# Dilated-attention scores as half-height products, with phase ends and first transfers reordered

## Chip, cores and metric

One core of a Trainium2 chip runs the whole program. The metric is device time in microseconds (us) of one execution; lower is better. Before the change three runs took 2113.09, 2116.16 and 2117.09 us, so the median is 2116.16.

## What is computed

The input x has 512 tokens of 1024 features. Two blocks follow each other.

The first block has two layers. In each, `p = rms_norm(x) @ w_in` gives the inputs of a latent attention (8 heads) and of a dilated attention, both gated with silu, and `x = x + concat(a, b) @ w_out`. The dilated attention has three groups of 8 heads of 64 features, with (window, dilation) of (128, 1), (512, 4) and (2048, 16). For each group

```
s = where(|qpos - kpos| <= half, q . k * 64 ** -0.5, -inf)
o, lse = softmax(s) @ v, logsumexp(s)
```

and the three outputs are mixed with `softmax(lse)` over the groups. A rotary embedding turns the first 16 features of each head of q and k.

The second block is an FFN, a mixer (a gated linear recurrence beside a window attention with sinks) and another FFN, each closed by an rms norm and added to the residual. All matrices are f32, and the result must be near the f32 reference.

## The kernel before

**Layout.** Activations lie with features on the 128 partitions and the 512 tokens along the row, so a 1024-feature matrix is eight tiles of 128 x 512. Weights stream in as 128 x 1024 pieces (`weights`, lines 129 to 143): a transfer on SP's queue, a cast to F32R on ACT (`hi`), and the rest `lo` on DVE. A product at nearly f32 precision is three F32R products, hi x hi, hi x lo and lo x hi (`mm3`, line 147). F32R runs in one pass, F32 in two.

**Order.** A scheduler places the instructions of each engine when the kernel is built. It goes by priorities (`high_priority`), by the order of the program and by modelled times; on the chip each engine then runs its list in order. `behind` adds an order without a wait. PSUM has eight banks of 128 x 512; `banks` (line 87) says which of them serve which kind of tile (`mm` projections, `s` scores, `t` transposes, `o` values), and each kind takes its banks in turn.

**Dilated attention** (in `layer`, lines 455 to 469). Heads go in four pairs, and a pair's two heads are the two halves of the 128 partitions. `dil_proj` makes q and k of three groups with six projections of 24 products. For group 0 and each head, the query tile `Qs[h]` holds the hi part on the head's own 64 partitions and the lo part on the other 64, and the keys `Kh[h]`, `Kl[h]` hold the head's keys twice, copied by eight transfers on SP's queue (line 702). So one product over 128 partitions sums hi and lo. For groups 1 and 2 the key tile `KP` has for each head its keys on its own half and zeros on the other (lines 709 to 712), so that the full query tile meets one head alone. `dil_scores` then makes, for each of four query blocks n and two heads h, one bank `s`: 256 columns of group 0 (lines 731 and 732, F32R) and 128 each of groups 1 and 2 (line 734, F32). DVE adds the mask and takes the maximum (line 739), and ACT takes the exponential (line 742). There is one `s` bank and three `t` banks. `dil_finish` scales, transposes (line 779) and copies (line 780) the probabilities, in turns put between the products of the next pair's last projection, and multiplies them with the values (line 784), head by head onto 64 columns of the array. The last pair of a layer is finished in `out`, among the first products of `w_out`.

**Phase ends** (`finish`, lines 279 to 334). The last output tiles (two in `end` and in `mixer`, one in `ffn`) are made in two halves of 256 tokens, A and B, in the same PSUM bank. `take` squares and copies a half; `stats` sums the squares with products against ones; `norm` runs a chain of small DVE operations for the reciprocal root; `spread` transposes it into a row R; `update` applies it, and the next phase's first projections (`follow`) run on half A while B is still being finished. `stats(0)` and `norm(0)` stand ahead of B's products in the program, `spread(0)` among the last tile's.

**Start.** WARM products on a tile of ones run first. SP's queue loads the vector table `vecs`, the x tile 0, then the weights and x tiles 4 to 7; ACT's queue loads x tiles 1 to 3. `take_x` casts an x tile on ACT, takes the rest on DVE, and squares it on ACT.

**Window attention** (`swa`, lines 1039 to 1053). Four tiles of values V, 24 products each, are made first; after the second the row R is made from `rstd` by four transposes, and keys and queries are scaled by R.

Of the kernel before, what the change touches and what calls it, by code (L numbers as in the profile page):

```python
# [22 lines left out]
P = 128  # L23
D = 1024
KT = 8
# [7 lines left out]
WARM = 6  # L33
# [11 lines left out]
class Kern:  # L45
    def __init__(self, ctx, tc, a, out):
# [18 lines left out]
        with tc.high_priority(1000):  # L65
            nc.sync.dma_start(self.vecs, a["vecs"])
# [212 lines left out]
    def finish(self, ms, prod, take, acc, update, srcs):  # L279


        pss = [self.psum() for _ in ms]
# [3 lines left out]
        def products(part, mid=None):  # L286
            for m, ps in zip(ms, pss):
                prod(m, ps, part, mid if m == ms[-1] else None)
            for m, ps in zip(ms, pss):
                take(m, ps, part)  # L290
# [17 lines left out]
        stats(0)  # L308
        norm(0)
        products(B, lambda: spread(0))  # L310
# [31 lines left out]
class Block1:  # L342
    def __init__(self, k, es):
# [12 lines left out]
        for kt in range(KT):  # L356
            x = self.u("x", F32)
            with tc.high_priority(1000 if kt < 4 else 0):
                (nc.scalar if 0 < kt < 4 else nc.sync).dma_start(x, a["xT"][kt])
            k.take_x(kt, x, k.vcol("norm_g0", kt), acc, sq=x)  # L360
# [13 lines left out]
    def layer(self, L):  # L374
# [84 lines left out]
        k.banks(mm=(0, 1, 2), s=(3,), t=(4, 5, 6), o=(7,))  # L459
# [211 lines left out]
    def dil_proj(self, L, pr, between=()):  # L671
# [4 lines left out]
        for g in range(3):  # L676
            for qk in range(2):
# [6 lines left out]
                if g == 0 and qk == 0:  # L684
                    ve.tensor_add(m1, m1, sh)
                    Qs = [self.q2("Qs", F32R) for _ in range(2)]
                    for h in range(2):
                        b, b2 = slice(64 * h, 64 * h + 64), slice(64 - 64 * h, 128 - 64 * h)
                        q = Qs[h].rearrange("p (t r i) -> p r t i", t=4, r=4)
                        m = m1.rearrange("p (r t i) -> p r t i", r=4, t=4)  # L690
                        nc.scalar.copy(q[b], m[b])
                        ve.tensor_sub(q[b2], m[b], q[b].bitcast(F32))
                elif g == 0:
                    ve.tensor_add(m1, m1, sh)
                    Kh, Kl = [[self.u("K0") for _ in range(2)] for _ in range(2)]
                    both = self.u("K0h"), self.u("K0l")
                    k.split(*both, m1)
                    for src, dst in zip(both, (Kh, Kl)):
                        for h in range(2):
                            b = slice(64 * h, 64 * h + 64)  # L700
# [189 lines left out]
def ffn(k, acc, lead, n, hd, after, srcs):  # L890
# [5 lines left out]
    with k.tc.tile_pool(name=f"ffn{n}", bufs=FT, reuse_waits="tile") as gp:  # L896
# [14 lines left out]
        def prod(m, ps, part, mid=None):  # L911
            for kt in range(FT):
                if mid and kt == FT // 2:
                    mid()
# [472 lines left out]
```

## Time and profile before

| | us |
|---|---|
| median of 3 runs | 2116.16 |
| profiled execution | 2112.34 |
| span of the profile | 2110.6 |
| PE busy | 2082.5 |
| DVE busy | 1328.4 |
| ACT busy | 963.3 |
| POOL busy | 94.8 |

The span goes from the first to the last instruction; the profiled execution took 1.74 us more than that. PE is the matmul engine, PEld its weight loads, DVE the vector engine, ACT the scalar engine, POOL the general one, SP an engine that mainly issues transfers. The time of a matmul in a row is from its start to the end of its last result; matmuls overlap, so their pitch is read from one start to the next.

### The profile page before, as it was taken

Reading aid. Unit: us, or ns where it says so; the run is one execution under the profiler, and the core shown is the slowest. Engines: PE = TensorE matmul, PEld = TensorE weight load, DVE = VectorE, ACT = ScalarE, POOL = GpSimd, SP = SyncE. Lnnn points to the kernel's source line nnn. Section 1 sums busy time; section 2 is a strip of 40 time slices with the busy share of each in tenths; the row PEclk is TensorE's granted clock in tenths of the full one; section 3 lists DMA queues with packets and bytes.
Section 4 is the critical chain, followed back from the end, with each engine's and each line's share of the span. In section 5 each row is a group of like instructions: output and inputs, shape, how many; then the busy total and the mean of one; then the engine's idle time right before and its main releaser. Section 6 shows DMA issues by size and latency. Waiting matters only on the chain.

```text
span 2110.6 us, 30554 instructions
## 1 busy us (share of the span) xinstructions
PE 2082.5 (99%) x11602; PEld 1763.0 (84%) x11602; DVE 1328.4 (63%) x2965; ACT 963.3 (46%) x1753; POOL 94.8 (4%) x350
## 2 busy tenths in 40 slices
PE   8999999999999999999999999999999999999997
PEld 7888889888888898788888889777888888888887
DVE  5866874856767757676555226866788748555323
ACT  5754444544664535543233224655577444223221
POOL 0000211100001201100000000000000000000001
PEclk9999999999999999999999999999999999999999
DMA  4323333433223343244222323322222434322221
GB/s 170 97 66 94 100 93 108 131 120 114 68 81 91 90 124 112 77 140 149 100 92 99 100 98 107 116 81 70 75 89 97 148 106 155 100 94 96 100 99 61
DMA packets 83780, 216.76 MB, mean 103 GB/s; under 512 B 9873, under 2 KB 28977, under 8 KB 83633
## 3 DMA queue, kind: packets, MB, share of 16 engines
q1 hardware_dynamic: 80896, 210.88, 31.1%
q10 hardware_dynamic: 2736, 3.93, 0.5%
q8 instruction: 91, 1.49, 0.3%
q14 instruction: 57, 0.46, 0.1%
HBM read 190.92 MB, written 13.37 MB: 97 GB/s over the span
## 4 chain that ended last, share of the span: by engine, by line
PE 90%; DVE 5%; ACT 2%; DMA 1%; issue 1%; SPq 0%; POOL 0%; DVEq 0%; ACTq 0%
PE ps L149 25%; PE ps L151 25%; PE ps L150 25%; PE ps L177 4%; PE ps L582 1%; PE ps L573 1%; PE ps L734 1%; PE ps L784 1%; PE ps L779 1%; PE ps L556 1%; DVE wl L142 1%; PE ps L557 1%; PE ps L558 1%; PE ps L1135 1%; PE ps L1119 0%
## 5 line engine op out<-in xcount | busy, mean ns | idle before, releaser
L141 ACT CAST wh<-wr 128x1024 fp32r<-128x1024 f32 (+2 forms) x341 | 343.4, 1009 | 682.8 <-PE ps L150 549.2
L149 PE MATMUL ps<-xh,wh 128*128 128x512 f32 x1496 | 592.0, 396 | 0.0
L142 DVE TENSOR_TENSOR wl<-wr,wh 128x1024 fp32r<-128x1024 f32 (+2 forms) x341 | 398.5, 1171 | 301.6 <-ACT wh L141 301.0
L150 PE MATMUL ps<-xl,wh 128*128 128x512 f32 x1496 | 587.4, 393 | 0.0
L151 PE MATMUL ps<-xh,wl 128*128 128x512 f32 x1496 | 587.3, 393 | 0.0
L151 PEld LDWEIGHTS ps<-xh,wl 128*128 128x128 f32 x1496 | 281.4, 188 | 56.4 <-issue 0.6
L149 PEld LDWEIGHTS ps<-xh,wh 128*128 128x128 f32 x1496 | 281.5, 188 | 54.6 <-issue 1.5
L150 PEld LDWEIGHTS ps<-xl,wh 128*128 128x128 f32 x1496 | 281.6, 188 | 52.7 <-issue 0.2
L149 PE MATMUL ps<-gh,wh 128*128 128x512 f32 (+1 forms) x540 | 199.3, 369 | 1.5 <-ACT f L939 1.5
L151 PE MATMUL ps<-gh,wl 128*128 128x512 f32 (+1 forms) x540 | 197.7, 367 | 0.7 <-DVE wl L142 0.7
L150 PE MATMUL ps<-gl,wh 128*128 128x512 f32 (+1 forms) x540 | 197.8, 366 | 0.5 <-DVE gl L191 0.5
L149 PE MATMUL ps<-wh,xh 128*128 128x256 f32 (+1 forms) x416 | 119.3, 287 | 0.2 <-ACT V L662 0.2
L150 PE MATMUL ps<-wl,xh 128*128 128x256 f32 (+1 forms) x416 | 118.9, 286 | 0.0
L151 PE MATMUL ps<-wh,xl 128*128 128x256 f32 (+1 forms) x416 | 118.8, 286 | 0.0
L149 PEld LDWEIGHTS ps<-gh,wh 128*128 128x128 f32 x540 | 101.9, 189 | 19.0 <-ACT f L939 1.9
L151 PEld LDWEIGHTS ps<-gh,wl 128*128 128x128 f32 x540 | 101.9, 189 | 18.0 <-DVE wl L142 1.6
L150 PEld LDWEIGHTS ps<-gl,wh 128*128 128x128 f32 x540 | 101.9, 189 | 16.9 <-DVE gl L191 0.9
L903 DVE TENSOR_TENSOR x<-ps,R 128x512 f32<-128x512 f32 x44 | 30.4, 690 | 98.4 <-PE ps L151 98.4
L901 DVE TENSOR_TENSOR x<-ps,R 128x512 f32<-128x512 f32 x44 | 30.4, 691 | 82.5 <-PE ps L151 81.2
L149 PEld LDWEIGHTS ps<-wh,xh 128*128 128x128 f32 x416 | 79.6, 191 | 1.5 <-ACT V L662 0.6
L150 PEld LDWEIGHTS ps<-wl,xh 128*128 128x128 f32 x416 | 79.5, 191 | 0.4 <-issue 0.2
L151 PEld LDWEIGHTS ps<-wh,xl 128*128 128x128 f32 x416 | 79.5, 191 | 0.4 <-issue 0.2
(303 smaller groups left out, 3247.5 us busy)
## 6 DMA issues: line engine op xcount, KB each, us to landing
wr<-in_ffn_w SPq DMA_DIRECT2D x132, 512.0 KB, 3.4
wr<-in_w_dqk SPq DMA_DIRECT2D x48, 512.0 KB, 3.6
wr<-in_w_dv SPq DMA_DIRECT2D x20, 512.0 KB, 3.5
wr<-in_w_out SPq DMA_DIRECT2D x16, 512.0 KB, 3.6
wr<-in_w_bgate SPq DMA_DIRECT2D x16, 512.0 KB, 3.5
hd<-h SPq DMA_DIRECT2D x48, 128.0 KB, 2.1
h<-hd SPq DMA_DIRECT2D x24, 256.0 KB, 5.5
wr<-in_w_gatea SPq DMA_DIRECT2D x8, 512.0 KB, 3.9
```

The lines of the kernel that those rows point to most:

```text
L141: nc.scalar.copy(hi[:, b:e], w[:, b:e])
L142: nc.vector.tensor_sub(lo[:, b:e], w[:, b:e], hi[:, b:e].bitcast(F32))
L149: first = mm(out, lhsT=wh, rhs=xh, start=start, stop=False)
L150: mm(out, lhsT=wh, rhs=xl, start=False, stop=False)
L151: return first, mm(out, lhsT=wl, rhs=xh, start=False, stop=stop)
L177: self.begin(mm(ps[:, part], lhsT=w[i][:, c], rhs=x[kt][:, part], start=start, stop=kt == KT - 1 and x is self.xl), ps.offset, start)
L556: mm(s, lhsT=qh[0:96, c], rhs=Kh[0:96, h, :], start=True, stop=False)
L557: mm(s, lhsT=qh[0:96, c], rhs=Kl[0:96, h, :], start=False, stop=False)
L558: mm(s, lhsT=ql[0:96, c], rhs=Kh[0:96, h, :], start=False, stop=True)
L573: turned[0] = inst(nc.tensor.transpose(t[:, j * P:(j + 1) * P], p[:, j * P:(j + 1) * P], k.ident))
L901: nc.vector.tensor_mul(x1, ps1, R)
L903: nc.vector.tensor_mul(x3, ps3, R)
```

## The change

Group 0's queries and keys are kept as hi and lo tiles with both heads on their own halves, and a score is three F32R products over 64 partitions: hi x hi, lo x hi, hi x lo. Groups 1 and 2 use the plain query and key tiles, one F32 product over 64 partitions for each head. The doubled keys, their eight transfers, the zero-filled tiles and their memsets are gone. Products are issued for two query blocks at once, alternating between the heads' halves, the second block first. Scores get four banks, of which two are shared with the transposes, which have two instead of three.

In `finish` a single last tile gets a bank for each half; sums and small chain of half A move among B's products, and the spread further back. In the first transfers `vecs` goes to ACT's queue, x tiles 2 and 3 to SP's without their priority, and the handling of x tile 0 gets priority; WARM goes from 6 to 8. In `swa` the row R is made after the third values tile. The changed `mtile` call below is that of `end`; the one of `mixer` differs in the names alone. The changed loop over kt is that of `ffn`, and the last lines are those of `swa`.

```diff
-WARM = 6
+WARM = 8
...
-            nc.sync.dma_start(self.vecs, a["vecs"])
+            nc.scalar.dma_start(self.vecs, a["vecs"])
...
     def finish(self, ms, prod, take, acc, update, srcs):
-        pss = [self.psum() for _ in ms]
+        pss = [(p, p) if len(ms) > 1 else (p, self.psum()) for p in (self.psum() for _ in ms)]
...
-        def products(part, mid=None):
+        def products(part, works=()):
+
+            for i, m in enumerate(ms):
+                prod(m, pss[i][part == B], part, works if len(ms) == 1 else works[i:i + 1])
             for m, ps in zip(ms, pss):
-                prod(m, ps, part, mid if m == ms[-1] else None)
-            for m, ps in zip(ms, pss):
-                take(m, ps, part)
+                take(m, ps[part == B], part)
...
         products(A)
-        stats(0)
-        norm(0)
-        products(B, lambda: spread(0))
+        products(B, (lambda: (stats(0), norm(0)), lambda: spread(0)))
...
             x = self.u("x", F32)
-            with tc.high_priority(1000 if kt < 4 else 0):
-                (nc.scalar if 0 < kt < 4 else nc.sync).dma_start(x, a["xT"][kt])
-            k.take_x(kt, x, k.vcol("norm_g0", kt), acc, sq=x)
+            with tc.high_priority(1000 if kt < 2 else 0):
+                (nc.scalar if kt == 1 else nc.sync).dma_start(x, a["xT"][kt])
+            with tc.high_priority(0 if kt else 500):
+                k.take_x(kt, x, k.vcol("norm_g0", kt), acc, sq=x)
...
-        k.banks(mm=(0, 1, 2), s=(3,), t=(4, 5, 6), o=(7,))
+        k.banks(mm=(0, 1, 2), s=(3, 6, 4, 5), t=(4, 5), o=(7,))
...
-                if g == 0 and qk == 0:
-                    ve.tensor_add(m1, m1, sh)
-                    Qs = [self.q2("Qs", F32R) for _ in range(2)]
-                    for h in range(2):
-                        b, b2 = slice(64 * h, 64 * h + 64), slice(64 - 64 * h, 128 - 64 * h)
-                        q = Qs[h].rearrange("p (t r i) -> p r t i", t=4, r=4)
-                        m = m1.rearrange("p (r t i) -> p r t i", r=4, t=4)
-                        nc.scalar.copy(q[b], m[b])
-                        ve.tensor_sub(q[b2], m[b], q[b].bitcast(F32))
-                elif g == 0:
-                    ve.tensor_add(m1, m1, sh)
-                    Kh, Kl = [[self.u("K0") for _ in range(2)] for _ in range(2)]
-                    both = self.u("K0h"), self.u("K0l")
-                    k.split(*both, m1)
-                    for src, dst in zip(both, (Kh, Kl)):
-                        for h in range(2):
-                            b = slice(64 * h, 64 * h + 64)
-                            for b2 in (slice(0, 64), slice(64, 128)):
-                                nc.sync.dma_start(dst[h][b2, :].bitcast(F32), src[b, :].bitcast(F32))
-                elif qk == 0:
-                    q = self.q2("Q12", F32)
-                    ve.tensor_add(q, m1, sh)
-                    Q12.append(q)
+                if g:
+                    z = self.q2("Q12", F32) if qk == 0 else self.u("K12", F32)
+                    ve.tensor_add(z, m1, sh)
+                    (K12 if qk else Q12).append(z)
+                    continue
+                ve.tensor_add(m1, m1, sh)
+                if qk:
+                    K0 = self.u("K0h"), self.u("K0l")
+                    k.split(*K0, m1)
                 else:
-                    kp = self.k4("KP", F32)
-                    nc.gpsimd.memset(kp[64:128, 0, :], 0.0)
-                    nc.gpsimd.memset(kp[0:64, 1, :], 0.0)
-                    ve.tensor_add(kp[0:64, 0, :], m1[0:64, :], sh[0:64, :])
-                    ve.tensor_add(kp[64:128, 1, :], m1[64:128, :], sh[64:128, :])
-                    K12.append(kp)
+                    Q0 = self.q2("Q0h", F32R), self.q2("Q0l", F32R)
+                    k.split(*(z.rearrange("p (t r i) -> p r t i", t=4, r=4) for z in Q0),
+                            m1.rearrange("p (r t i) -> p r t i", r=4, t=4))
...
+        rows = slice(0, 64), slice(64, 128)
+
+        def scores(n, ss, first):
+
+            c = slice(n * P, (n + 1) * P)
+
+            def win(z):
+                return z.rearrange("p (r i) -> p r i", r=4)[:, :, WIN[n]:WIN[n] + 64]
+
+            for i, (q, kk) in enumerate(((qh, kh), (ql, kh), (qh, kl))):
+                for s, b in zip(ss, rows):
+                    ins = mm(s[:, 0:256], lhsT=q[b, c], rhs=win(kk)[b], start=i == 0, stop=i == 2)
+                    first = k.behind(inst(ins), first)
+            for g in range(2):
+                for s, b in zip(ss, rows):
+                    ins = mm(s[:, 256 + g * P:256 + (g + 1) * P], lhsT=Q12[g][b, c], rhs=K12[g][b, c], start=True, stop=True)
+                    first = k.behind(inst(ins), first)
+            return first
+
+        two = {}
         for n in range(4):
-            c = slice(n * P, (n + 1) * P)
-            for h in range(2):
-                s = k.bank("s")
-                win = [z[h].rearrange("p (r i) -> p r i", r=4)[:, :, WIN[n]:WIN[n] + 64] for z in (Kh, Kl)]
-                mm(s[:, 0:256], lhsT=Qs[h][:, c], rhs=win[0], start=True, stop=False)
-                mm(s[:, 0:256], lhsT=Qs[h][:, c], rhs=win[1], start=False, stop=True)
-                for g in range(2):
-                    mm(s[:, 256 + g * P:256 + (g + 1) * P], lhsT=Q12[g][:, c], rhs=K12[g][:, h, c], start=True, stop=True)
+            if n % 2 == 0:
+                two = {m: [k.bank("s") for h in range(2)][::-1] for m in (n, n + 1)}
+                first = None
+                rows = rows[::-1]
+                for m in (n + 1, n):
+                    first = scores(m, two[m], first)
+                rows = rows[::-1]
+            ss = two[n][::-1]
+            for h, s in enumerate(ss):
...
-            k.mtile(ws[m], 0, gh, gl, range(KT), ps, part=part, between=[mid] if mid else ())
+            k.mtile(ws[m], 0, gh, gl, range(KT), ps, part=part, between=[lambda: None, *works])
...
             for kt in range(FT):
-                if mid and kt == FT // 2:
-                    mid()
+                for work in works[kt // 10:kt // 10 + 1] if kt % 10 == 5 else ():
+                    work()
...
-            if t == 1:
+            if t == 2:
                 k.R = k.row(rstd, "R")
```

## Rows read from the trace of the kernel before

**Rows 1.** The page: busy time per engine, and the chain that ended last by engine.

```profile
PE 2082.5 (99%) x11602; PEld 1763.0 (84%) x11602; DVE 1328.4 (63%) x2965; ACT 963.3 (46%) x1753; POOL 94.8 (4%) x350
...
PE 90%; DVE 5%; ACT 2%; DMA 1%; issue 1%; SPq 0%; POOL 0%; DVEq 0%; ACTq 0%
```

**Rows 2.** Groups by line, shapes apart; columns as in part 5 of the page.

```profile
L734 PE MATMUL ps<-KP,Q 128*128 128x128 f32 x256 | 39.6, 275 | 0.9 <-DVE KP L711 0.9
...
L731 PE MATMUL ps<-K,Qs 128*128 128x256 f32 x64 | 18.6, 291 | 0.3 <-DVE mx L739 0.2
...
L779 PEld LDWEIGHTS ps<-ident,p 128*128 128x128 f32 x256 | 31.6, 140 | 8.4 <-DVE p L777 0.4
...
L784 PEld LDWEIGHTS ps<-PT,V 128*64 128x64 f32 x512 | 27.8, 137 | 1.3 <-issue 1.3
```

**Rows 3.** Timeline of PE, one score tile: start, us, engine, line, operation, count.

```profile
220.39 0.28 PE L731 MATMUL ps<-K,Qs 128*128 128x256 f32 x1
220.50 0.28 PE L732 MATMUL ps<-K,Qs 128*128 128x256 f32 x1
220.62 0.61 PE L734 MATMUL ps<-KP,Q 128*128 128x128 f32 x4
220.98 0.47 PE L151 MATMUL ps<-xh,wl 128*128 128x512 f32 x1
221.30 0.39 PE L149 MATMUL ps<-xh,wh 128*128 128x512 f32 x1
```

**Rows 4.** Timeline of PE, the end of layer 0: transposes, value products, output projection.

```profile
427.81 1.47 PE L779 MATMUL ps<-ident,p 128*128 128x128 f32 x12
429.21 3.71 PE L784 MATMUL ps<-PT,V 128*64 128x128 f32 x64
432.86 0.50 PE L149 MATMUL ps<-gh,wh 128*128 128x512 f32 x1
433.20 0.40 PE L150 MATMUL ps<-gl,wh 128*128 128x512 f32 x1
```

**Rows 5.** Groups by line, DVE and ACT around the dilated scores.

```profile
L739 DVE CUSTOM_DVE_ANT_0 p<-ps,mask 128x256 f32<-128x256 f32 x128 | 49.0, 420 | 20.3 <-PE ps L734 20.1
...
L780 ACT COPY PT<-ps 128x512 f32<-128x512 f32 x64 | 37.3, 589 | 33.2 <-PE ps L779 33.1
...
L712 DVE TENSOR_TENSOR KP<-m,sh 64x512 f32<-64x512 f32 x16 | 11.0, 689 | 0.4
L705 DVE TENSOR_TENSOR Q<-m,sh 128x512 f32<-128x512 f32 x16 | 11.0, 687 | 0.1
...
L711 DVE TENSOR_TENSOR KP<-m,sh 64x512 f32<-64x512 f32 x16 | 10.8, 674 | 0.0
```

**Rows 6.** Busy time by engine, 212.8 to 270, dilated stage: stretch, us, busy (count).

```profile
212.80:270.00 57.20, 57.04 (x345) 47.77 (x344) 46.61 (x137) 27.91 (x60) 11.59 (x38) 1.00 0.30 89
```

**Rows 7.** Timeline of PE, layer 1, the last pair's first scores; the wait in brackets.

```profile
852.68 0.46 PE L734 MATMUL ps<-KP,Q 128*128 128x128 f32 x2 [0.87 <-DVE KP L711]
```

**Rows 8.** Timeline of PE, the ends of Block1 and of the second FFN.

```profile
919.01 0.61 PE L223 MATMUL ps<-ones,sq 128*128 128x1 f32 x4 [0.25 <-DVE sq L251]
...
2089.10 0.28 PE L151 MATMUL ps<-gh,wl 128*128 128x256 f32 x1
2090.12 0.39 PE L149 MATMUL ps<-gh,wh 128*128 128x256 f32 x1 [0.74 <-ACT f L939]
```

**Rows 9.** Timeline of ACT and PE, the first ten microseconds.

```profile
5.84 0.40 ACT L141 CAST wh<-wr 128x256 fp32r<-128x256 f32 x1 [3.61 <-DMA wr<-in_w_lat]
...
8.05 0.72 ACT L190 ACTIVATE xh<-x,vecs 128x512 fp32r<-128x512 f32 x1
...
8.82 1.65 PE L177 MATMUL ps<-xh,wh 128*128 128x512 f32 x3 [4.85 <-ACT xh L190]
```

**Rows 10.** Timeline of PE, the mixer's window attention, before the row R.

```profile
1322.93 0.28 PE L151 MATMUL ps<-wh,xl 128*128 128x256 f32 x1
1325.44 0.65 PE L232 MATMUL ps<-ident,rstd 128*128 128x128 f32 x4 [2.23 <-DVE rstd L213]
```

More of the change, by code (lines that the diff above doesn't have):

```diff
@@ L714, in dil_proj @@
-        return Qs, Kh, Kl, Q12, K12
+                if g:
[7 more added lines that the diff above has]
+                    k.split(*K0, m1)
+                else:
+                    Q0 = self.q2("Q0h", F32R), self.q2("Q0l", F32R)
+                    k.split(*(z.rearrange("p (t r i) -> p r t i", t=4, r=4) for z in Q0),
+                            m1.rearrange("p (r t i) -> p r t i", r=4, t=4))
@@ L716, in dil_scores @@
+        return Q0, K0, Q12, K12
     def dil_scores(self, proj):
@@ L719, in dil_scores @@
         ve, mm = nc.vector, nc.tensor.matmul
-        Qs, Kh, Kl, Q12, K12 = proj
+        (qh, ql), (kh, kl), Q12, K12 = proj
         own, oth, ps = k.small("own", 32, 2), k.small("oth", 32, 2), []
@@ L854, in end, with prod @@
         xs, hs, acc, ws = [None] * KT, [None] * KT, [], {}
-        def prod(m, ps, part, mid=None):
+        def prod(m, ps, part, works=()):
             if m not in ws:
                 ws[m] = k.weights(a[f"w_out{L}"][m])
-            k.mtile(ws[m], 0, gh, gl, range(KT), ps, part=part, between=[mid] if mid else ())
+            k.mtile(ws[m], 0, gh, gl, range(KT), ps, part=part, between=[lambda: None, *works])
         def take(m, ps, part):
@@ L909, in ffn, with prod @@
         ws = {}
-        def prod(m, ps, part, mid=None):
+        def prod(m, ps, part, works=()):
             for kt in range(FT):
-                if mid and kt == FT // 2:
-                    mid()
+                for work in works[kt // 10:kt // 10 + 1] if kt % 10 == 5 else ():
+                    work()
                 b = m * FT + kt
@@ L993, in mixer, with prod @@
         ws, xh, xl = {}, k.xh, k.xl
-        def prod(m, ps, part, mid=None):
+        def prod(m, ps, part, works=()):
             if m not in ws:
                 ws[m] = k.weights(a["w_o"][m])
-            k.mtile(ws[m], 0, xh, xl, range(KT), ps, part=part, between=[mid] if mid else ())
+            k.mtile(ws[m], 0, xh, xl, range(KT), ps, part=part, between=[lambda: None, *works])
         def tile_(name):
```

## The prediction

> **What bounds the kernel now.** I read the page first. TensorE (PE) is busy 99% of the span and carries 90% of the chain that ended last; VectorE (DVE) carries 5% [rows 1]. The kernel is a row of matmuls, so a change is worth the PE time that it removes plus the PE waits that it closes. Work on DVE, ACT and the queues counts only where PE waits for it.
>
> Next I took the groups by line for the score products that the change rewrites. The F32 products of line 734 appear 256 times for 128 calls: an F32 product is two passes. Line 731 appears 64 times, in one pass, because it is F32R [rows 2]; line 732 is its twin. So there are 64 score tiles (2 layers, 4 pairs, 4 query blocks, 2 heads), and each has two passes of 256 columns and four of 128.
>
> The PE timeline of one tile gives its price. It starts at 220.39. The next projection product starts at 220.98 and the one behind it at 221.30 instead of the usual 0.23 us later [rows 3]. So the tile holds PE for 0.91 - 0.23 = 0.68 us: 0.11 and 0.12 for the F32R passes, 0.11 for each F32 pass (four are busy 0.61 and one lasts 0.275, so (0.61 - 0.275) / 3; the last is partly hidden behind the next product), and about 0.09 for coming back from F32 to F32R. 64 x 0.68 = **43.5 us** in all, which is the pot that the main edit draws from.
>
> **Does a half of the array run beside the other half?** No product of the kernel before takes 64 of the 128 rows. The nearest rows are the value products, which split the columns: each fills 64 columns of the array and the two heads alternate. Twelve full transposes of 128 columns take 1.40 us to the next start, or 0.117 each; 64 value passes of the same 128 columns take 3.65 us, or 0.057 each [rows 4]. One could say that half as many weight columns simply load in half the time, but the loads last 140 and 137 ns [rows 2], nearly alike. So I read it as two column halves side by side. For row halves the two bounds are "together as column halves do" and "one after the other". I take "together": a full product already moves 128 rows per column, and two halves move 64 rows each, so they read no more than now. What is new is that both write all 128 partitions, into two banks; no row shows that.
>
> **Scores, part by part.** A burst after the change covers two query blocks and two heads, four tiles: 12 F32R passes of 256 columns and 16 F32 passes of 128. With overlap that is 6 x 0.117 + 8 x 0.111 = 1.59 us. The two passes of one head cannot overlap each other, so a burst ends with about one single pass, 0.11. Going into the split form and back costs something too: before the value products the start is 0.09 late (one transpose per (1.47 - 0.27) / 11 = 0.109, so 1.31 of the 1.40), and after them the first full product takes 0.34 instead of 0.23, so 0.11 [rows 4]. Sum 1.59 + 0.11 + 0.20 = 1.90 us per burst, 16 bursts, 30.4 us. **Gain 43.5 - 30.4 = 13.1 us.** Without overlap a burst is 12 x 0.117 + 16 x 0.111 + 0.20 = 3.38 us, 54.1 in all: 10.6 us slower. With no tail and no switch it is 25.4 us, a gain of 18.1.
>
> [...]
>
> **What DVE, ACT, POOL and the queues lose.** Per pair DVE drops four half-height key additions (0.674 and 0.689, twice) and two half-height query subtractions (like line 712), 4.1 us, and gains two full-height additions and one subtraction at the price of line 705, 0.687 each, 2.1 us [rows 5]. ACT drops one of two casts, POOL four memsets, and the SP queue eight copies of K0. In this stage DVE is busy 46.6 of 57.2 us against 57.0 for PE [rows 6], so these sit beside PE's work and I count them as nothing, but for one place: in the last pair of layer 1 PE waits 0.87 us for the half-height key addition [rows 7]. One addition of 0.69 replaces two in a row, so **0.7 us** goes (0 to 0.9). If that cover were gone, the 2 us per pair would count, a further 16 us; I see no reason for it, since PE is the longer one.
>
> **The waits that it adds.** The score tiles now turn over four banks, and the transposes of the softmax two instead of three, and banks 4 and 5 belong to both. A second burst waits until DVE has read all four tiles of the first; all later products stand behind it, since PE runs in order. DVE needs per tile two reads of 0.42 [rows 5] and, as I estimate, about half as much again for the small operations behind them, about 1.3 us, 5.3 for four. Two projections of 24 products at 0.23 us can stand in between, 11 us. I count no wait; one tile's 1.3 us at each of the 8 second bursts, 10.6 us, is the other bound. Transposes wait for a copy of 0.589 [rows 5] two turns back instead of three. Where three turns stand without anything between [rows 4] the third would wait some 0.25 us, once per layer: **+0.5 us** (0 to 4, if every pair did so twice).
>
> **Phase ends.** In each FFN the second half of the last output's columns goes to the bank that ACT still reads: the product at 2090.12 starts 1.02 us after the last instead of 0.12 [rows 8], 0.9 lost, and the same again in the other FFN. Another bank ends this. The sums and the small DVE chain, now put at the sixth of 22 steps, and the transposes, at the sixteenth, stay behind work. In the second FFN DVE is late next (the first half's updates are still in its queue), so I take 0.9 + 0.5 = **1.4 us** (0 to 1.8). In the first block's end and the mixer the sums wait 0.25 [rows 8]; three products more in front of them give **0.4 us** (0 to 1).
>
> **Start.** PE idles 4.85 us until the first x tile is cast. That cast starts at 8.05 behind three weight casts on ACT, the first of which started at 5.84 when its weights landed [rows 9]. With the x cast ahead of them the first product can start at 5.84 + 0.40 = 6.24, 2.6 earlier. ACT now issues the vector load and one x tile instead of three; SP loses the vector load ahead of x and takes two x tiles behind the six weight parts, and these are wanted only after 18 products. The x square, also moved up, may take 0.6 us ahead of a weight cast. I take **2.3 us** (0 to 4, the upper end if weights land sooner as well). Two more warm-up products fill idle time and cost nothing.
>
> **Row of R in the mixer.** PE waits 2.23 us (2.5 from start to start) for the reciprocal root [rows 10]. The third values tile, 24 products at 0.12, or 2.9 us, now stands in front and fills it. But R comes no earlier, and DVE's work on keys and queries follows it, so part of the wait comes back at the first scores: **1.2 us** (0 to 2.4).
>
> **Sum.** 13.1 + 0.7 - 0.5 + 1.4 + 0.4 + 2.3 + 1.2 = 18.6 us. The profiled execution took 2112.3 us (span 2110.6), so 2093.7 by itself; the median of the runs is 2116.2, 3.8 above it, and so I say **2097.5 us**. A measurement of this kernel can tell about 0.2%, or 4.2 us, from no change.
>
> **The rivals.**
> *No overlap of the row halves* (slower). Its place is the 16 bursts, its price 10.6 us against the other gains of 5.5: 2116.2 + 5.1 = 2121 us. It decides from a burst of 3.06 us on. For it speaks that PSUM writes double; against it, the column halves. Chance 0.09.
> *DVE becomes the bound of the bursts.* Four tiles arrive at once, and DVE is 81% busy already [rows 6]. Each second burst waits for one tile, 10.6 us: 2108 us. Against it stands DVE's relief of 2 us per pair. Chance 0.12. [...]
> *More than I count*: no tail at the bursts, the whole start and the whole wait for R. 18.1 + 0.9 + 1.8 + 1 + 4 + 2.4 = 28 us: 2088. Chance 0.09.
> *The forecast*, 0.70, by itself 2090 to 2105.
>
> **Numbers.** The range takes in the upper gain and the DVE rival, 2087 to 2110. Faster: the forecast, the larger gain and most of the DVE rival, 0.86. Same: the rest of that rival and a mild form of no overlap, 0.07. Slower: 0.07.
>
> **What would show it.** Right: start times of the score products in pairs a few ns apart, a burst near 1.9 us, its next product about 0.1 late; the first projection product near 6.5 us; no wait of 0.74 in the FFN ends. Wrong: score passes evenly 0.11 apart (no overlap), or idle PE before a burst released by the score reads on DVE.

## The result and the profile after

The changed kernel takes 2100.82 us (median of 4 runs, 2100.36 to 2101.46) against 2115.34 for the kernel before in 4 runs (2113.09 to 2117.09). The ratio is 0.9941, interval 0.9929 to 0.9953: faster by 0.6%, 14.5 us by the medians. The forecast was 18.6 us less and 2097.5 us. The profiled execution after took 2101.13 us (span 2098.9), 11.7 us of span less than the profiled one of before. In the experiments, on three chips, the kernel before had medians of 2113.27, 2113.27 and 2113.28, and the changed kernel, run again on the third, 2100.16. So 11.7 to 13.1 us is the better figure for the gain.

The page of the changed kernel, its busy times and its chain by engine, answering to [rows 1]:

```profile
PE 2071.4 (99%) x11670; PEld 1747.3 (83%) x11670; DVE 1304.8 (62%) x2941; ACT 954.1 (45%) x1745; POOL 72.9 (3%) x318
...
PE 89%; DVE 5%; ACT 2%; DMA 1%; issue 1%; SPq 0%; ACTq 0%; DVEq 0%
```

PE, busy for 99% of the span and 89% of that chain, still bounds the kernel. It lost 11.1 us of busy time; DVE lost 23.6 and POOL 21.9, which lay beside it.

A first burst of the dilated scores (layer 0, the second pair) on the timeline of PE, answering to [rows 3]:

```profile
261.38 0.39 PE L151 MATMUL ps<-xh,wl 128*128 128x512 f32 x1
261.69 0.39 PE L720 MATMUL ps<-K0h,Q0h 64*128 64x256 f32 x2
261.92 0.28 PE L720 MATMUL ps<-K0h,Q0l 64*128 64x256 f32 x2
262.04 0.28 PE L720 MATMUL ps<-K0l,Q0h 64*128 64x256 f32 x2
262.15 0.61 PE L724 MATMUL ps<-K,Q 64*128 64x128 f32 x8
262.51 0.36 PE L720 MATMUL ps<-K0h,Q0h 64*128 64x256 f32 x2
...
262.95 0.61 PE L724 MATMUL ps<-K,Q 64*128 64x128 f32 x8
263.49 0.50 PE L149 MATMUL ps<-xh,wh 128*128 128x512 f32 x1
263.83 0.40 PE L150 MATMUL ps<-xl,wh 128*128 128x512 f32 x1
```

Every entry counts two products, or eight F32 passes, and yet the next starts after the time of one or four: 0.12 us behind the pair at 261.92, where a single pass of before took 0.12. The two products of a pair start 3 to 6 ns apart. So the two halves of the array run side by side here. Four tiles take 1.80 us to the next product. The burst starts 0.31 after the last projection product and the second product behind it stands 0.34 after the first, instead of 0.23, so a burst holds PE for 1.80 + 0.08 + 0.11 = 1.99 us. The forecast had 1.90.

If every pair took no longer than one pass, a burst would take 1.59 us. It takes 0.40 more, in four places of about 0.1 each: the late start (0.31), the first pair (0.23 to the next instead of 0.12), the last one (from 262.95 to 263.49, or 0.54 for four passes of 0.108), and the product behind the next (0.34).

The second burst of the same pair:

```profile
267.29 0.39 PE L150 MATMUL ps<-xl,wh 128*128 128x512 f32 x1
268.44 0.39 PE L720 MATMUL ps<-K0h,Q0h 64*128 64x256 f32 x2 [0.76 <-DVE mx L743]
```

It starts 1.15 us after the product before it instead of 0.31. The list of PE's waits (us in total, times, longest) says how often that happens, and what else is new:

```profile
PE ps L232 <- DVE rstd L213: 5.5, 4, 2.9
PE ps L720 <- DVE mx L743: 3.9, 5, 0.9
...
PE ps L223 <- ACT sq L247: 1.4, 2, 1.0
PE ps L724 <- DVE K L686: 1.1, 2, 0.6
...
PE ps L783 <- ACT PT L784: 0.5, 2, 0.2
```

Five of the eight second bursts wait, 3.9 us in all; by start times four lose 0.83 us and one 0.94, 4.3 together. In the first pair of each layer the F32 products also wait for a key addition of group 1 or 2. There the burst splits in two, and PE goes in and out of the split form twice. The wait of [rows 7] is gone. The timeline of DVE shows why the second burst is late:

```profile
262.66 1.23 DVE L142 TENSOR_TENSOR wl<-wr,wh 128x1024 fp32r<-128x1024 f32 x1 [0.17 <-ACT wh L141]
263.80 0.69 DVE L479 SCALAR_TENSOR_TENSOR g<-th,gs 128x512 f32<-128x512 f32 x1
264.52 0.69 DVE L430 TENSOR_TENSOR g<-g 128x512 f32<-128x512 f32 x1
265.13 0.42 DVE L743 CUSTOM_DVE_ANT_0 p<-ps,mask 128x256 f32<-128x256 f32 x1
...
267.96 0.42 DVE L743 CUSTOM_DVE_ANT_0 p<-ps,mask 128x256 f32<-128x256 f32 x1
```

The first burst ends on PE at 263.49. DVE first does a weight's rest and two gate operations and begins to read at 265.13; eight reads take until 268.38, and the second burst starts at 268.44. It had been put some 0.8 us too early, behind 17 projection products. In the stretch of [rows 6] PE is now idle for 1.3 us and DVE has become lighter:

```profile
212.80:270.00 57.20, 55.87 (x371) 46.06 (x371) 43.45 (x141) 27.69 (x65) 9.66 (x40) 1.00 0.23 75
```

The start, timeline of ACT and PE, against [rows 9], and the first sums over x, which stood at 27.53 us before:

```profile
3.87 0.72 ACT L190 ACTIVATE xh<-x,vecs 128x512 fp32r<-128x512 f32 x1 [1.19 <-DMA vecs<-in_vecs]
4.57 0.40 ACT L141 CAST wh<-wr 128x256 fp32r<-128x256 f32 x1
5.03 1.59 PE L177 MATMUL ps<-xh,wh 128*128 128x512 f32 x2 [0.19 <-ACT wh L141]
...
10.51 1.48 PE L177 MATMUL ps<-xh,wh 128*128 128x512 f32 x3
11.79 1.48 PE L177 MATMUL ps<-xh,wl 128*128 128x512 f32 x3
...
26.05 0.95 PE L223 MATMUL ps<-ones,x 128*128 128x1 f32 x8
```

The first product starts 3.8 us earlier, but of this only 1.5 is left at the sums. Three products take 1.28 us at 10.51, or 0.43 each, where the usual is 0.23. In experiment 4 a product takes as long where the granted clock is 0.51; here the profile gives a clock of 1.00 from 5.3 to 13.2 us, so it does not show what slows these products. PE gets to the usual 0.23 only at 13.2 us (before: 13.7).

By start times of the same instructions in the two profiles: the start gains 1.5 us, the two dilated layers 4.5 and 4.6, the end of the first FFN 1.0, the row R nothing that lasts; the end of the mixer loses 0.9, the second FFN gains 1.0 and the tail loses 0.5. With 0.5 in small shifts up to the window attention that makes the 11.7 us.

### The profile page after: what moved, and what is told of

It is laid out like the page before. It is cut to its first block, busy times and chain, and to the rows that moved or that the text cites. A ratio compares the mean times of both kernels' runs of the same rounds, so it can differ in the third digit from the quotient of the medians.

```text
span 2098.9 us, 30465 instructions
## 1 busy us (share of the span) xinstructions
PE 2071.4 (99%) x11670; PEld 1747.3 (83%) x11670; DVE 1304.8 (62%) x2941; ACT 954.1 (45%) x1745; POOL 72.9 (3%) x318
## 4 chain that ended last, share of the span: by engine, by line
PE 89%; DVE 5%; ACT 2%; DMA 1%; issue 1%; SPq 0%; ACTq 0%; DVEq 0%
PE ps L151 25%; PE ps L149 25%; PE ps L150 25%; PE ps L177 4%; PE ps L582 1%; PE ps L573 1%; PE ps L783 1%; PE ps L788 1%; DVE wl L142 1%; PE ps L556 1%; PE ps L557 1%; PE ps L558 1%; DVE p L743 1%; ACT wh L141 1%; PE ps L1139 1%
## 5 line engine op out<-in xcount | busy, mean ns | idle before, releaser
L907 DVE TENSOR_TENSOR x<-ps,R 128x512 f32<-128x512 f32 x44 | 30.4, 690 | 98.2 <-PE ps L151 98.2
L905 DVE TENSOR_TENSOR x<-ps,R 128x512 f32<-128x512 f32 x44 | 30.4, 690 | 82.5 <-PE ps L151 81.2
L669 POOL COPY oth<-own 32x4 f32<-32x4 f32 x256 | 56.8, 222 | 692.0 <-ACT p L746 682.6
```

The costliest lines, as they stand in the source:

```text
L669: self.mover.tensor_copy(dst[32 * b:32 * b + 32, a:a + 1], src[32 * a:32 * a + 32, b:b + 1])
L905: nc.vector.tensor_mul(x1, ps1, R)
L907: nc.vector.tensor_mul(x3, ps3, R)
```

## The experiments

The first four ran on one chip (before: 2113.27 us), the next four on a second (2113.27), the last three on a third (2113.28).

**1. The heads one after the other.** Same products and banks; a tile is finished on one half before the other head's starts.

```diff
-            for i, (q, kk) in enumerate(((qh, kh), (ql, kh), (qh, kl))):
-                for s, b in zip(ss, rows):
+            for s, b in zip(ss, rows):
+                for i, (q, kk) in enumerate(((qh, kh), (ql, kh), (qh, kl))):
...
-            for g in range(2):
-                for s, b in zip(ss, rows):
+                for g in range(2):
```

> The changed kernel with the same score products in another order: all five of one head, then all five of the other, so neighbours on PE use the same half of the array. Theory (the gain comes from the two halves running side by side): a tile takes 3 x 0.117 + 4 x 0.111 = 0.80 us by itself, four tiles 3.2 instead of the 1.80 measured, so 16 x 1.4 = 22 us more, 2116 to 2124 us. Rival (the gain comes from the dropped key copies, memsets and half-height additions): the order does not matter, within 3 us of 2100.8.

Measured: 2109.53 us, ratio 0.9981 (0.9972 to 0.9990), some 9 us slower than the change. The direction was right, the size was not: part of the overlap survives. Its timeline shows where:

```profile
260.77 0.39 PE L720 MATMUL ps<-K0h,Q0h 64*128 64x256 f32 x1
...
261.23 0.27 PE L723 MATMUL ps<-K,Q 64*128 64x128 f32 x1
261.24 0.38 PE L720 MATMUL ps<-K0h,Q0h 64*128 64x256 f32 x1
...
262.62 0.61 PE L723 MATMUL ps<-K,Q 64*128 64x128 f32 x4
263.16 0.50 PE L149 MATMUL ps<-xh,wh 128*128 128x512 f32 x1
```

The next tile's F32R products on the other half start at 261.24, while F32 passes of the tile before start until 261.56. The burst takes 2.39 us; the single passes laid end to end, by the durations that the prediction used, would be 12 x 0.117 + 16 x 0.111 = 3.18. So here a half went on with its own row of products while the other was busy with the other type, and alternating the heads is worth 0.59 us a burst, 9.4 us over 16. The second bursts, coming later, start only 0.28 us late instead of 0.83, so by start times the two layers lose 7.9 us and not 9.4; that the whole runs also differ by some 9 is in part chance.

**2. The scores alone.** The kernel before with only the dilated part of the change (projections, scores, banks).

```diff
-        k.banks(mm=(0, 1, 2), s=(3,), t=(4, 5, 6), o=(7,))
+        k.banks(mm=(0, 1, 2), s=(3, 6, 4, 5), t=(4, 5), o=(7,))
...
-        return Qs, Kh, Kl, Q12, K12
+        return Q0, K0, Q12, K12
```

> The kernel before with the dilated scores and their banks alone changed. Theory: the dilated stages give 9.5 us of the 14.5, as the traces of before and after stand apart there, so 2105 to 2107 us. Rival (start, phase ends and the later row of R give most): 2110 us or more.

Measured: 2104.99 us, 0.9957 (0.9943 to 0.9971), 8.3 us less. The dilated part brings 8 to 9 us, not the 13.3 of the prediction (13.1 + 0.7 - 0.5).

**3. A higher priority for the score reads on DVE.** If DVE's other work stands ahead of the reads, a higher priority for them should close the waits.

```diff
-                    ve.tensor_tensor_reduce(out=p[:, d], in0=s[:, d], in1=self.mask[:, 4 * i or n, :], scale=1.0,
+                    with k.tc.high_priority(200):
+                        ve.tensor_tensor_reduce(out=p[:, d], in0=s[:, d], in1=self.mask[:, 4 * i or n, :], scale=1.0,
```

> The changed kernel with a higher priority for DVE's reads of the score banks (mask and maximum), so that they stand ahead of gate and weight work. Theory (PE waits some 0.9 us before each second burst because DVE begins the four reads 1.6 us late, behind other work): the waits of line 720 on line 743, 3.9 us by the profile and 0.9 from start to start each, go, and the kernel takes 2094 to 2097 us. Rival (DVE is full in this stage, so what is put back is missed elsewhere): 2100 to 2103 us, with waits for weights or projections in place of these.

Measured: 2105.95 us, 0.9957 (0.9945 to 0.9970): 5 us slower than the change. A miss. The waits are the same, as its list of PE's waits says:

```profile
PE ps L720 <- DVE mx L744: 4.0, 5, 0.9
PE ps L149 <- ACT gh L190: 1.8, 1, 1.8
```

The priority did not put the reads ahead of the other work. The first burst ends on PE at 262.06, and the timeline of DVE has the first read:

```profile
263.70 0.42 DVE L744 CUSTOM_DVE_ANT_0 p<-ps,mask 128x256 f32<-128x256 f32 x1
```

It starts 1.64 us behind the burst as in the change, after the same weight's rest and two gate operations. The reads only stand closer, mostly 0.34 us apart instead of 0.41, and the second burst comes after 16 projection products instead of 17, so the wait stayed. What reads ahead of that work would give was thus not tried. New waits came up elsewhere, 1.8 us for `gh` among them, and in two short stretches, 1317.8 to 1321.0 and 1727.4 to 1730.0 us, the granted clock was 0.50.

**4. Blocks, banks and halves in natural order.** The change issues the second block first, with the heads and their banks reversed; here all three stand as they are counted.

```diff
-                two = {m: [k.bank("s") for h in range(2)][::-1] for m in (n, n + 1)}
+                two = {m: [k.bank("s") for h in range(2)] for m in (n, n + 1)}
...
-                rows = rows[::-1]
-                for m in (n + 1, n):
+                for m in (n, n + 1):
```

> The changed kernel with the two query blocks of a burst in their natural order, the first block first. Theory (taking the block whose bank is read last first makes PE wait for all four reads; in natural order the first block needs two only): no wait before the second burst, but the products fall into bursts of one block, 16 more switches at 0.2 to 0.3 us, 3 to 5 us back for 6 to 7 us saved: 2097 to 2100 us. Rival (a burst of one block costs as much as one of two, 1.8 us, or PE waits within): 2104 us or more.

Measured: 2124.02 us, 1.0041 (1.0027 to 1.0055): 23 us slower than the change, and slower than the kernel before. The expectation was badly missed. The second burst falls apart into single tiles:

```profile
265.60 0.38 PE L720 MATMUL ps<-K0h,Q0h 64*128 64x256 f32 x1 [0.99 <-DVE mx L741]
...
267.18 0.38 PE L720 MATMUL ps<-K0h,Q0h 64*128 64x256 f32 x1
...
267.64 0.60 PE L724 MATMUL ps<-K,Q 64*128 64x128 f32 x4
```

From 265.60 the tiles stand about 0.8 us apart, the time in which the change does two: banks come free one by one, and nothing is left to pair with. Its list of waits has ten for the score reads, 7.1 us, instead of five. Behind it the granted clock falls from 1.00 (260 to 268 us) to 0.51; busy time by engine and, after the five engines, the granted clock:

```profile
268.00:275.00 7.00, 7.00 (x21) 5.35 (x20) 3.56 (x26) 6.86 (x24) 4.32 (x24) 0.51 0.00 0
```

For 7 us PE has 0.51, and the same follows in layer 1 from 728.9 to 735.8; a product takes 0.43 instead of 0.23 (271.70 to 272.13). Ahead of the first stretch PE had waited 0.99 us and run single tiles. By an estimate from 7 us at 0.51 these two stretches cost about 3.4 us each, the waits for score reads 3.2 more than in the change. By start times the two layers lose 23.3 us against the change, so the whole loss lies there; how the rest of it divides between lost pairs and clock is not settled. The order of the blocks and of the banks belongs to the edit as much as the halves do.

**5. The second burst later.** To move the burst instead of the reads, its first product is ordered behind an instruction that comes later, the last exponential of the first four tiles. This is order alone; no wait is added on the chip.

```diff
-                    nc.scalar.activation(p[:, d], p[:, d], AF.Exp, bias=nm, scale=nsc[i][:, n:n + 1],
-                                         accum_out=sv[:, i, n, 1, h:h + 1])
+                    late = inst(nc.scalar.activation(p[:, d], p[:, d], AF.Exp, bias=nm, scale=nsc[i][:, n:n + 1],
+                                                     accum_out=sv[:, i, n, 1, h:h + 1]))
...
-                first = None
+                first = late
```

> The changed kernel with the second burst of a pair ordered, for the scheduler alone and without a semaphore, behind the last exponential of the first four tiles, so that four more projection products stand ahead of it. Theory (the scheduler puts the burst some 0.9 us before DVE has read the fourth tile, so PE stands idle with work behind it): six waits of 0.9 and the short one go, 4 to 6 us less, ratio to before 0.991 to 0.992 where the changed kernel has 0.9941. Rival (the products put in between come from a place where PE then waits): ratio 0.994 to 0.995.

Measured: 2098.22 us, 0.9927 (0.9915 to 0.9940), the lowest median of all versions. The waits are gone:

```profile
267.14 0.39 PE L150 MATMUL ps<-xl,wh 128*128 128x512 f32 x1
267.45 0.39 PE L720 MATMUL ps<-K0h,Q0h 64*128 64x256 f32 x2
```

The burst starts 0.31 after the product before it, and its list of waits has no line for the score reads any more. Against experiment 8, which is as good as the change on the same chip, 2.8 us are gained of the 4.3 that the five waits cost: in the two layers the profile shows 2.0 less, as part comes back at the layers' ends. The expectation had 4 to 6 us less. 23 projection products now stand between the two bursts instead of 17. That the waits came from where the burst stands is shown; that DVE lacks the time for the reads is not so, since it does the same work here.

**6. The old first transfers**, with six warm-up products.

```diff
-WARM = 8
+WARM = 6
...
-            nc.scalar.dma_start(self.vecs, a["vecs"])
+            nc.sync.dma_start(self.vecs, a["vecs"])
...
-            with tc.high_priority(0 if kt else 500):
+            if True:
```

> The changed kernel with the first transfers, the priority of x tile 0 and the six warm-up products of the kernel before. Theory: the start is worth 1.5 to 3.1 us, as the first sums of the profiles show, so 2102.3 to 2104 us where the changed kernel has 2100.8. Rival (an earlier first product is lost again to the clock and to late weights): within 0.8 us of the changed kernel.

Measured: 2105.69 us, 0.9962 (0.9950 to 0.9975), 4.7 us more than experiment 8 and above the expected 2102.3 to 2104. In its profile the first sums stand at 27.14 us, against 24.25 in experiment 8: 2.9 us come from the start. Its profile then loses another 2.9 between the mixer's gate and its output projection, where PE waits 1.9 us for `lr` (0.5 in experiment 8) and a stretch of 3.4 us at a granted clock of 0.51 follows (1644.2 to 1647.6). What that has to do with the first transfers was not tried. PE also waits 1.5 to 2.0 us for `lr` in experiments 4, 7 and 10, which have the new start, so 2.9 us is the safer price of the start.

**7. The old ends of the phases.**

```diff
-        products(B, (lambda: (stats(0), norm(0)), lambda: spread(0)))
+        stats(0)
+        norm(0)
+        products(B, lambda: spread(0))
```

> The changed kernel with the phase ends of the kernel before: one bank for both halves, sums and small chain ahead of the second half. Theory: the two FFN ends lose 0.9 us each again, the mixer's end gains 0.9 back, so +1 us, 2101 to 2102.5 us. Rival (each part as forecast, the mixer's wait being chance): +1.8 to +2.5 us.

Measured: 2101.07 us, 0.9945 (0.9932 to 0.9957), the same as the change. Two lines of its list of PE's waits say why:

```profile
PE ps L149 <- ACT f L944: 1.5, 2, 0.7
PE ps L223 <- ACT sq L247: 0.5, 1, 0.5
```

The two waits of [rows 8] for ACT are back, and the wait of 0.96 us at the mixer's end is gone. The new ends win in the FFNs what they lose in the mixer.

**8. The row R after the second values tile, as before.**

```diff
-            if t == 2:
+            if t == 1:
```

> The changed kernel with the row R made after the second values tile again. Theory (DVE's chain after R paces the first scores, so the wait only moves): within 0.7 us of the changed kernel. Rival (the values tile in front is gained outright, as I forecast in part): 1.2 to 2.4 us more.

Measured: 2101.03 us, 0.9940 (0.9927 to 0.9954): the edit is worth nothing. In this version and in the change, as before, 48 values products stand ahead of the four transposes and 48 behind; the place in the program doesn't decide where they go. The change's own row:

```profile
1313.23 0.65 PE L232 MATMUL ps<-ident,rstd 128*128 128x128 f32 x4 [1.79 <-DVE rstd L213]
```

**9. The change again**, on the third chip, unedited, to see how much one profile differs from the next.

> The changed kernel as it is, beside the two below on one chip. Theory: the ratio of 0.9941 again within its interval, and an FFN end without a wait; the first sums anywhere from 24 to 26 us, as the profiles of the same start differ. Rival (the start's 1.5 us spread belongs to the program): 26.0 us again.

Measured: 2100.16 us, 0.9941 (0.9929 to 0.9954), as the first time. But its first sums stand at 24.15 us, 1.9 earlier than in the first profile of the same kernel. Its first products come 0.23 us apart by 8.8 us:

```profile
8.80 0.84 PE L177 MATMUL ps<-xh,wh 128*128 128x512 f32 x3
9.48 0.84 PE L177 MATMUL ps<-xh,wl 128*128 128x512 f32 x3
```

Three products in 0.68 us, where the first profile has 1.28. What the start is worth thus differs between the executions: 1.5 or 3.4 us by these two. Of the ten profiles with the new start, nine have their first sums between 24.1 and 24.7 us; the three with the old one have them between 27.1 and 27.7. So about 3 us is usual, and the first profile of the change is the exception.

The same profile loses 1.5 us against the first one behind the mixer's end: after the same wait of 0.96 us the granted clock is 0.50 from 1719.1 on.

```profile
1719.10:1722.50 3.40, 3.40 (x18) 3.40 (x17) 3.36 (x12) 2.25 (x6) 0.00 (x0) 0.50 0.70 234
```

**10. Experiment 5 with the old ends where two tiles are last** (mixer and first block), to keep the FFNs' gain without the mixer's loss.

```diff
+        if len(ms) > 1:
+            stats(0)
+            norm(0)
+            products(B, (lambda: None, lambda: spread(0)))
+        else:
+            products(B, (lambda: (stats(0), norm(0)), lambda: spread(0)))
```

> The kernel of e5 (second burst later) with the ends of the two-tile phases (first block, mixer) as before, those of the FFNs as changed. Theory (the mixer's new wait of 1.1 us between the sums comes from the sums being put among the second half's products): 0.7 to 1.3 us less than e5, the FFN gain kept, ratio 0.991 to 0.9925. Rival (that wait is the order on ACT by chance, a weight cast ahead of the square, and the end has other waits in place): within 0.5 us of e5.

Measured: 2099.57 us, 0.9938 (0.9925 to 0.9950), no better than experiment 5. The wait at the mixer's end stays:

```profile
PE ps L223 <- ACT sq L247: 1.2, 2, 1.0
```

So the place of the sums is not its cause. The timeline of PE shows the mixer's last sums, first before:

```profile
1731.62 0.50 PE L223 MATMUL ps<-ones,sq 128*128 128x1 f32 x4
1732.25 0.62 PE L177 MATMUL ps<-xh,wh 128*128 128x256 f32 x3
...
1733.54 0.54 PE L223 MATMUL ps<-ones,sq 128*128 128x1 f32 x4
```

In the change:

```profile
1719.51 0.50 PE L223 MATMUL ps<-ones,sq 128*128 128x1 f32 x4
1720.97 0.61 PE L223 MATMUL ps<-ones,sq 128*128 128x1 f32 x4 [0.96 <-ACT sq L247]
```

Before, and in experiment 7, ten first products of the next phase stand between the two groups of sums and cover the square on ACT, which stands behind a weight cast in all of these versions. In the change and in experiment 10 those ten stand behind both groups, as ACT casts their x tile only after the square (in the change at 1721.07 us, the square at 1720.54). Of the changed end, experiment 10 keeps the place of the spread, three products further back than before. That this moved them is likely, but was not tried by itself.

**11. Experiment 5 with R after the fourth values tile.**

```diff
-            if t == 2:
+            if t == 3:
```

> The kernel of e5 with the row R made after the fourth values tile. Theory (keys and queries wait for R on DVE, and DVE paces the first scores): no wait before the row, but the first scores come as late as in e5 or later, 0 to 1 us more. Rival (PE's wait is what costs): 1.5 to 2 us less than e5.

Measured: 2098.70 us, 0.9932 (0.9918 to 0.9945), the same as experiment 5. The wait before the four transposes is 1.98 us there, and here too 48 values products stand ahead of them and 48 behind. So neither this experiment nor number 8 moved the row on PE; what it would be worth behind more products was not tried.

By whole runs the parts add up: 8.3 (experiment 2) + 4.7 (6) + 0 (7) + 0 (8) = 13.0 us, and the whole change gave 2113.28 - 2100.16 = 13.1 on the third chip. That they meet so closely is in part luck, since the 4.7 holds more than the start; with its 2.9 they make 11.2.

## Why the prediction held, and which step failed

**Overlap of the row halves: right.** The value products' column halves were the right neighbour. The rival "no overlap" (2121 us) falls: four tiles take 1.80 us against 3.18 laid end to end, 1.77 times.

**Size of a burst: right within 0.1 us, by two errors.** The tail of 0.11 does not exist: the two heads' F32 passes run in step to the end, eight in 0.54 us at 262.95. Instead the switch in and out costs 0.40 and not the 0.20 of the sum. The prediction read it off the start of the value products and the product behind the next, and these two came out as forecast (0.08 and 0.11). The first pair and the last one are about 0.1 longer as well. In the value products of [rows 4] the last pair also takes 0.20 to the next product instead of 0.10, but that lay hidden in the 3.65 us that were divided by 64. What PE does in these 0.4 us the rows do not tell.

**"I count no wait": this step failed.** The prediction gave 11 us of products to cover 5.3 us of DVE work and concluded that the second burst finds its banks free. That is a statement on how much work there is. What decided is where the burst was put: the order is fixed ahead, 17 products stand between the bursts and not the 48 that could (23 in experiment 5), and DVE starts on the scores 1.6 us after the burst ends, behind gate and weight work. Idle PE before a burst, released by the score reads, is also what the prediction itself named as a sign of being wrong. Those five waits make 4.3 us. The two waits for group keys are 0.64 each (the burst starts 0.96 after the product before it instead of 0.32), and with the second switch a split burst costs 1.05 more, 2.1 for both.

The terms can be counted over all bursts in the two traces, as the time from the product ahead to the second one behind, less two usual pitches of 0.23 us. After the change the scores hold PE for 38.0 us: the 30.4 of the sum, 1.4 for bursts of 1.99 instead of 1.90, 4.3 and 2.1 for the waits, less 0.2 for two bursts right behind value products. Before it they held PE for 46.6 us and not 43.5, since 1.2 went to the key addition of [rows 7], where the prediction has 0.7, and 1.9 to split tiles and other short waits. So the scores gave 8.6 us where the sum had 13.8; with the 0.5 that the transposes were to cost, 13.3. By the profiles the two layers gave 9.1 us (8.3 in experiment 2).

Of the rival "DVE becomes the bound of the bursts" this is the milder half: the waits of it came, at five of eight places and at less than half of the price, 4.3 instead of 10.6 us. But experiment 5 shows that DVE's reads of the scores were not the limit: with the burst moved, the same reads no longer appear in the list of PE's waits, where they had 3.9 us.

**The transposes' two banks: right in kind.** Forecast 0.5 us; the list of waits has 0.5 in two. From start to start the last twelve transposes of a layer take 1.86 us instead of 1.40, which is 0.9 for both layers.

**KP wait of [rows 7]: right.** It is gone, but a wait for a key addition came back in the first pair of each layer, where it was not looked for.

**Phase ends: half right.** The waits of 0.9 in the FFNs closed as forecast: the first FFN gains 1.0, and the second 1.0 less 0.5 in the tail. Products now follow there with 0.36 us and the sums between them:

```profile
2079.70 0.28 PE L151 MATMUL ps<-gh,wl 128*128 128x256 f32 x1
2079.82 0.50 PE L223 MATMUL ps<-ones,sq 128*128 128x1 f32 x4
2080.18 0.36 PE L149 MATMUL ps<-gh,wh 128*128 128x256 f32 x1
```

The 0.4 us for the first block and the mixer came out as -0.9. At the first block's end the wait for the square is still there, 0.2 us, and in the mixer, where the list of before has no such wait, the last sums now wait 0.96 for a square that ACT does behind a weight cast, as the products that covered it have moved behind them (experiment 10). By whole runs the ends are worth 0 (experiment 7), not 1.8. In eight of the ten profiles with that wait a stretch at a granted clock of 0.50 follows it, so its price is often nearer 2.4 than 0.9 us, with the 1.5 that experiment 9 loses there. The prediction looked at what stands ahead of the sums on PE and not at what stands ahead of the square on ACT.

**Start: right in place and within its range.** 2.3 us forecast; 1.5 and 3.4 in two profiles of the changed kernel, about 3 in most of the others, 2.9 in experiment 6 against 8 and 4.7 there by whole runs. The first product came at 5.03 us, sooner than the 6.24 forecast, since the x cast now ends at 4.59 and the first weight cast starts at 4.57 without a wait. That the pace of the first products varies between executions, 0.43 and 0.23 us apart in the two profiles of the changed kernel, was not in the sum.

**Row R: wrong, 0 instead of 1.2.** The step said that a third tile now stands in front of the row. It doesn't; the order on PE is not the program's. The wait is 1.79 us instead of 2.23, and the difference is lost again before the window attention.

**The sum.** By the profiles the dilated part came 4.2 us short, the ends 1.2 (0.6 instead of 1.8), the row 1.2 and the start 0.8; with 0.5 us of small gains elsewhere, 18.6 becomes 11.7. The time itself was missed by 3.3 us only, and that is luck: the median that it was put on, 2116.2, stood 3 us above those of the kernel before in the experiments. From 2113.3 the same gain would have made 2094.7, 6.1 us off.

## What to carry to other kernels

In the changed kernel products over 64 partitions on alternate halves of the array ran side by side, F32R and F32 alike, four tiles in 1.80 us where the single passes laid end to end make 3.18: issue them in turn, half by half, with a bank for each. By these rows a pair can be priced like one product, with 0.4 us more a burst at its start and its end, half of it inside the burst. Where a scheduler places the work, a burst that reuses banks has to be checked for where it lands, not only for whether there is enough work to cover it; ordering it behind a later instruction (experiment 5) got back 2.8 of 4.3 us. Moving a line in such a program may move nothing on the engine (the row R in experiments 8 and 11), so look for the order in the trace before a price is put on it.

## What the runs showed of the hardware that was not expected

- In experiment 1 one half of the array worked on its own products while the other half was on an earlier tile, and with another type (F32R at 261.24 beside F32 at 261.23), so even heads in turn gained 3.18 - 2.39 = 0.8 us per burst. The loop of that version issues the product that starts at 261.24 behind both F32 products of the tile before, and passes of these start until 261.56. Whether PE left the order of its list there, other than is said for the kernel before, or the scheduler had put them in this order, the rows do not tell.
- In these profiles a stretch at a granted clock of 0.50 came behind some waits of PE and not behind others, and the length of the wait does not tell which. After the mixer's wait of 0.96 us, 3.4 us at 0.50 follow in eight of ten profiles, not in the first one of the change and that of experiment 5. After the row R they follow in six of thirteen: behind a wait of 1.98 us in experiment 11, and of 2.94 in experiment 7, below, but not behind 2.78 in experiment 1 or 2.23 before. In experiment 4, 7 us at 0.51 came twice, behind split bursts. By an estimate from the 0.50 (3.4 x 0.5) a stretch of 3.4 us costs 1.7 us, and experiment 9 lost 1.5, more than its wait of 0.96; what decides stays open.

```profile
1314.40:1317.80 3.40, 3.40 (x16) 3.40 (x17) 2.65 (x5) 2.57 (x5) 0.00 (x0) 0.50 0.91 264
```

- The first products of one and the same kernel came 0.43 us apart up to 13.2 us in one execution and 0.23 apart by 8.8 us in another, with the first sums 1.9 us earlier in the second.
